# A depthwise convolution moved wholly to TensorE as 128x32 products over shifted copies

## The chip, the cores and the metric

The kernel runs on one core of one Trainium2 chip. The metric is the device time of one execution in microseconds (us). Lower is better.

## The reference

The program is a small network over 256 tokens of width 1024: ten stages, of which six are feed-forward blocks and four are mixers (a convolution with windowed attention, forgetting attention, an mLSTM, a relative-position attention). The change concerns the convolution in the second stage, the "even" mixer:

```
z = h @ w_in                                # h [256, 1024]
u, gate = z[..., :512], z[..., 512:1024]
a = u * sigmoid(gate)                       # [256 tokens, 512 channels]
y = causal depthwise conv of a, 31 taps, weights w [31, 512], + b
a_out = silu(layernorm(y) * ln_g + ln_b)
b_out = windowed attention of 8 heads, from q, k, v = z[..., 1024:]
h = concat(a_out, b_out) @ w_out
```

Depthwise means that channel c of the output sums 31 shifted copies of channel c alone, each with its own factor. Everything is float32.

## The kernel before

**Tiling.** Tokens come in two blocks of 128, b = 0 and b = 1. Weights stream from DRAM in units of 128x2048 float32 (1 MB) into two buffers named `raw`; ACT rounds each half of a unit to a high part and DVE subtracts to get a low part (both `hl`, 20 buffers of 128x1024, so five units). A product of activations and weights is three TensorE matmuls (high by high, high by low, low by high), issued 512 columns wide. Small products (attention scores, transposes, the convolution) are plain float32: in the profile such a matmul stands as two instructions, here called halves; a transpose is one.

**The order of the work.** Each operation is recorded with an engine, an estimated duration, the tiles that it reads and writes, and a key (the unit of weights it belongs to, plus offsets). `Rec.schedule` plays a list schedule over PE, ACT, DVE and the DMA queue: among what is ready on an engine it takes the lowest key, and tiles get buffers as they come free. The table `NUDGE` shifts the keys of single groups ("even conv b0 p" is the PE work of the convolution of block 0) and so sets the order by hand. What comes out is one fixed order for each engine; every engine then runs in that order and waits on semaphores. All DMAs of the kernel are issued from one queue, SP's, in order too.

**The convolution** (`Net.even`, lines 1098 to 1271). After the gate, `a` is transposed to channels by tokens and copied into `aT` (two tiles, each with two of the four groups of 128 channels, `ct`, and 30 columns of zeros ahead of the tokens). The number `cg=6` splits the work. Of group 0 all 31 taps and of group 1 the last 15 are done on TensorE: one 128x128 diagonal matrix for each tap, loaded from DRAM (`in_diag`, 12 loads), times the shifted tokens. That makes 46 products for each token block, 92 in all. The other 16 taps of group 1 and all of groups 2 and 3 are done on DVE: 78 instructions over 256 tokens each, a multiply and add by a factor per channel (lines 1173 to 1184). The results are `yT`, which the layer norm ("even ln") transposes back.

**What stands around it.** The same stage does the projections, scores, softmax and value products of eight attention heads, and its output projection follows with attention's half of the sum first. `L273` in the profile is every matmul, `L277` every transpose, `L281` every load, `L207` every ACT operation, `L217`, `L236` and `L248` are DVE's tensor-tensor, scalar-tensor-tensor and min-reduce helpers.

Of the kernel before, what the change touches and what calls it, by code (L numbers as in the profile page):

```python
# [12 lines left out]
P = 128  # L13
# [59 lines left out]
class Rec:  # L73
# [191 lines left out]
    def mm(self, out, l, r, start, stop, key=None):  # L265
        n = self.n_of(r)
        if r.v.dt == F32R:
            d = max(107.0 if self.shape(l)[1] > 64 else 53.5, n / 2.4) + 2.5
        else:
            ls = self.shape(l)  # L270
            d = 126.0 if ls[1] == 64 else 2 * max(107.0, n / 1.2) + 4
        self.op("PE", d, [l, r], [out],
                lambda: self.nc.tensor.matmul(self.res(out), self.res(l), self.res(r), start=start, stop=stop), key=key)  # L273

    def tr(self, out, in_, ident, key=None):
        self.op("PE", 109.0, [in_, ident], [out],
                lambda: self.nc.tensor.transpose(self.res(out), self.res(in_), self.res(ident)), key=key)  # L277

    def load(self, out, src, nbytes, key=None, after=None):
        o = self.op("DMA", max(nbytes / 360.0 + 0, 453.0), [src], [out],  # L280
# [179 lines left out]
class Net:  # L460
# [74 lines left out]
    def rstd(self, ss, w, n, key, more=False, cut=1):  # L535
        """[P, w] sums of squares (parts of them) -> rsqrt(ss / n + eps), Newton from the exponent trick"""
# [29 lines left out]
    def split_T(self, src, n, hi, lo, key, o0=0, pk=None):  # L566
        """transposes n [128,128] blocks of src into hi + lo at column block o0"""
# [10 lines left out]
    def ssq(self, b, key):  # L578
        """sums of squares of the halves of x"""
# [7 lines left out]
    def gain_T(self, b, g, key):  # L587
        """x * g, transposed and split"""
# [26 lines left out]
    def norm(self, b, g):  # L615
        """(x * g).T in two parts, and per token 1 / rms, half of it, half its square"""
# [9 lines left out]
    def mm3(self, out, x, w, first, last, key):  # L626
        """out += x.T @ w from halves: groups of one k-block"""
# [6 lines left out]
    def proj(self, b, xs, us, u0, n, per, grp=2):  # L634
        """bank [128, n] = x @ W; units hold `per` k-blocks of n columns each"""
# [16 lines left out]
    def oproj(self, b, acc, hi, lo, o0, un, u0, first, last):  # L652
        """acc[2 banks] += o @ W; unit holds 2 k-blocks of 1024 columns"""
# [13 lines left out]
    def postnorm(self, b, acc, g, scale):  # L667
        """x += scale * rmsnorm(acc) * g"""
# [138 lines left out]
    def bias_tile(self, b, name, j, key):  # L807
        """additive bias of 4 heads of a query block: for one key block or two"""
# [14 lines left out]
    def k_T(self, b, kT, pt, key):  # L823
        """bank [128, 2 pairs x 128] -> kT [128, 2 pairs x 256]"""
# [4 lines left out]
    def qk_T(self, b, key, bank, rs, kT, sgn=1.0):  # L829
        """row-layout bank [tok, 512] -> (qT [128, nq*128] scaled, kT) via transposes"""  # L830
# [13 lines left out]
    def logsig(self, z, w, out, key):  # L844
        """out = min(z, 0) - log1p(exp(-|z|)), [P, w]"""
# [29 lines left out]
    def gates(self, b, xs, gu, u0, key):  # L875
        """bank [128, 16] = x @ W for 16 columns: W is the stationary side, the sum is turned afterwards"""
# [221 lines left out]
    def even(self, gi):  # L1098
# [12 lines left out]
        cw, cbi, lg, lb = c[:, 520:644], c[:, 644:648], c[:, 648:652], c[:, 652:656]  # L1111
# [3 lines left out]
        T2 = 30 + 2 * P  # L1115
        a2 = [r.t("aT", 2 * T2, name="aT") for _ in range(2)]
        y = r.t("b4", name="yT")
        ng = [min(4, max(0, int(self.c["cg"]) - 4 * ct)) for ct in range(4)]
        part = [None, None]

        def tap(ct, t0, n):
            o = (ct % 2) * T2 + t0
            return a2[ct // 2][:, o:o + n]

        for b in range(2):
# [14 lines left out]
            for i in range(2):  # L1140
                if b == 0:
                    r.begin()
                    for ct in (2 * i, 2 * i + 1):
                        r.memset(tap(ct, 0, 30), 0.0)
                    r.end(key)
                r.begin()
                for ct in (2 * i, 2 * i + 1):
                    r.copy(tap(ct, 30 + b * P, P), pt[:, ct * P:(ct + 1) * P])
                r.end(key)
            r.lab = f"even conv b{b}"  # L1150
            kp = self.pos(b, u0 + 3) - self.c["vp"]
            for ct in range(4):
                if ng[ct] == 0:
                    continue
                bank = r.t("mm", name="cv")
                for q in range(4 - ng[ct], 4):
                    n = min(8, 31 - 8 * q)
                    d = r.t("b4", n * P, name="diag")
                    at = u0 + self.c["lead"] * b + self.c["du"] + 4 * ct + q
# [5 lines left out]
                ys = y[:, (2 * ct + b) * P:(2 * ct + b + 1) * P]  # L1165
                if ng[ct] == 4:
                    r.act(ys, bank[:, 0:P], AF.Identity, bias=cbi[:, ct:ct + 1], key=kp)
                else:
                    part[b] = r.t("b1", name="part")
                    r.act(part[b][:, 0:P], bank[:, 0:P], AF.Copy, key=kp)  # L1170
        r.lab = "even conv"
        key = self.pos(1, u0 + 3) - self.c["vb"]
        for j in range(31):
            r.begin()
            for ct in range(3, -1, -1):
                if j >= 8 * (4 - ng[ct]):
                    continue
                ys = y[:, 2 * ct * P:2 * (ct + 1) * P]
                w = cw[:, ct * 31 + j:ct * 31 + j + 1]
                if j == 0:  # L1180
                    r.ts(ys, tap(ct, j, 2 * P), w, cbi[:, ct:ct + 1], ALU.mult, ALU.add)
                else:
                    r.stt(ys, tap(ct, j, 2 * P), w, ys, ALU.mult, ALU.add)
            r.end(key)
        for ct in range(4):
            if 0 < ng[ct] < 4:
                for b in range(2):
                    ys = y[:, (2 * ct + b) * P:(2 * ct + b + 1) * P]
                    r.tt(ys, part[b][:, 0:P], ys, ALU.add, key=key)
# [37 lines left out]
        for b in range(2):  # L1227
# [4 lines left out]
            for j in range(4):  # L1232
                r.tr(pt[:, j * P:(j + 1) * P], y[:, (2 * j + b) * P:(2 * j + b + 1) * P], self.ident)
# [236 lines left out]
def _cols(w, c0, n):  # L1470
    """[1024, cols] -> units of n-wide columns, 2048 // n k-blocks each: [units, 128, 2048]"""
# [4 lines left out]
def _rows(w):  # L1476
    """[K, 1024] -> units of two k-blocks: [K / 256, 128, 2048]"""
# [11 lines left out]
def arrange(i):  # L1489
# [50 lines left out]
    diag = np.zeros((4, P, 32, P), np.float32)  # L1540
    cwt = i["conv_w"][0].reshape(31, 4, P)
    for c in range(4):
        diag[c, np.arange(P), :31, np.arange(P)] = cwt[:, c].T
# [4 lines left out]
        x=i["x"][0], w=np.concatenate(w), wg5=gates(fx, 3072 + np.array(slot)), wg7=gates(ml), cst=cst, row=row, swab=tile4(swab), diag=diag.reshape(4, P, 4096),  # L1548
# [7 lines left out]
    g=(F32, 1024, 3, 0), aT=(F32, 572, 4, 0), b4=(F32, 1024, 5, 0), b2=(F32, 512, 11, 0), b1=(F32, 256, 6, 0), s=(F32, 32, 16, 0),  # L1556
    acc=(F32, 512, 4, 1), mm=(F32, 512, 4, 1))
CFG = dict(lead=4, ahead=0, cb=2, fb=6, dd=4, ab=3, vb=2, ncst=784, stages=99, rk=3, bl=3, cg=6, vp=0, du=4, nd=0, k4=2, xb=1, k2=1)

NUDGE = {  # L1560
# [88 lines left out]
```

## Time and profile before

| | |
|---|---|
| median of 3 runs | 1593.0 us (1592.84 to 1593.87) |
| span of the profiled execution (its own time, first to last instruction) | 1591.4 us |
| PE busy | 1573.6 us (99%), clock granted at full in every slice |
| DVE, ACT busy | 1015.5 us (64%), 837.4 us (53%) |
| weights and other loads | 296.83 MB, 16 DMA engines 51% busy |

The profile counts an engine as busy from the start of an instruction to its end, and matmuls overlap each other by some hundred ns. So the price of one more matmul in a row is read from the growth of a row's length with its count, not from the mean duration. A timeline row merges instructions of one kind that follow each other: start, length, engine, line, what it writes and reads, count, and in brackets the idle time ahead of it with what ended it.

### The profile page before, as it was taken

The page shows a single profiled execution, that of the slowest core. Times are in us where ns is not written, and L with a number is a line of the kernel's source. Part 1 is how long each engine was busy: PE and PEld are TensorE (multiplying, and loading weights), DVE is VectorE, ACT ScalarE, POOL GpSimd, SP SyncE. Part 2 cuts the span into 40 slices and gives each one's busy share as a digit, 9 for nine tenths or more (in the row PEclk, how much of TensorE's full clock was granted, in tenths as well). Part 3 has the DMA queues.
Part 4 walks back from the last instruction along what each step waited for, and adds up shares of the span by engine and source line. Part 5 has one row for each costly group of instructions (what it writes and reads, how often), then busy time and mean ns, then how long its engine had stood idle before and what let it go on. Part 6 is the DMA issues. An engine that isn't in the chain of part 4 may idle for free.

```text
span 1591.4 us, 20430 instructions
## 1 busy us (share of the span) xinstructions
PE 1573.6 (99%) x7714; PEld 1289.5 (81%) x7714; DVE 1015.5 (64%) x1969; ACT 837.4 (53%) x1400; POOL 0.2 (0%) x4
## 2 busy tenths in 40 slices
PE   8999999999999999999999999999999999999998
PEld 6888888888888888887788888788888887788886
DVE  6555689854558555677964557887545576755544
ACT  6444556744455454566854445655444457754443
POOL 0000000000000000000000000000000000000000
PEclk9999999999999999999999999999999999999999
DMA  6655585355554555446444554445544645354542
GB/s 244 217 185 211 176 299 184 117 184 188 215 215 151 210 185 211 161 179 208 169 161 183 204 219 160 146 146 198 199 175 169 238 173 202 142 185 185 208 175 80
DMA packets 49587, 296.83 MB, mean 187 GB/s; under 512 B 5408, under 2 KB 8912, under 8 KB 16720
## 3 DMA queue, kind: packets, MB, share of 16 engines
q1 hardware_dynamic: 49488, 295.52, 50.9%
q8 instruction: 60, 0.98, 0.2%
q14 instruction: 39, 0.32, 0.1%
HBM read 294.43 MB, written 1.07 MB: 186 GB/s over the span
## 4 chain that ended last, share of the span: by engine, by line
PE 93%; DVE 3%; DMA 2%; ACT 1%; issue 0%; SPq 0%; ACTq 0%; DVEq 0%
PE mm L273 60%; PE acc L273 28%; PE mm L277 5%; DMA raw<-in_w 2%; DVE hl L217 1%; DVE b L236 1%; ACT hl L207 1%; ACT b L207 1%; DMA x<-in_x 0%; DVE s L236 0%; DVE xt L236 0%; DVE b L248 0%; ACT xt L207 0%; DVE x L236 0%; SPq L281 0%
## 5 line engine op out<-in xcount | busy, mean ns | idle before, releaser
L273 PE MATMUL mm<-hl,xt 128*128 128x512 f32 (+1 forms) x4224 | 1013.0, 393 | 0.6 <-DVE xt L217 0.3
L273 PEld LDWEIGHTS mm<-hl,xt 128*128 128x128 f32 x4224 | 778.0, 188 | 161.4 <-DVE hl L217 2.2
L217 DVE TENSOR_TENSOR hl<-raw,hl 128x1024 fp32r<-128x1024 f32 (+1 forms) x518 | 618.0, 1213 | 350.2 <-ACT hl L207 259.5
L207 ACT ACTIVATE hl<-raw 128x1024 fp32r<-128x1024 f32 (+1 forms) x518 | 522.3, 1048 | 332.6 <-DMA raw<-in_w 168.1
L273 PE MATMUL acc<-hl,gt 128*128 128x512 f32 x1584 | 385.8, 393 | 0.0
L273 PEld LDWEIGHTS acc<-hl,gt 128*128 128x128 f32 x1584 | 293.1, 188 | 59.4 <-ACT gt L207 0.2
L207 ACT ACTIVATE b<-mm,s 128x256 f32<-128x256 f32 (+2 forms) x188 | 94.0, 509 | 219.9 <-PE mm L273 214.7
L236 DVE SCALAR_TENSOR_TENSOR b<-mm,s,b 128x256 f32<-128x256 f32 x132 | 63.3, 481 | 98.4 <-ACT b L207 98.1
L277 PE MATMUL mm<-cst,b 128*128 128x128 f32 (+1 forms) x680 | 109.4, 272 | 3.0 <-DVE s L248 2.5
L277 PEld LDWEIGHTS mm<-cst,b 128*128 128x128 f32 (+1 forms) x680 | 85.4, 140 | 32.2 <-ACT b L207 3.7
L207 ACT ACTIVATE gt<-mm 128x256 fp32r<-128x256 f32 x132 | 50.0, 378 | 92.1 <-PE mm L277 84.6
L273 PE MATMUL acc<-hl,xt 128*128 128x512 f32 x384 | 96.0, 397 | 0.7 <-DVE xt L217 0.7
L217 DVE TENSOR_TENSOR gt<-mm,gt 128x256 fp32r<-128x256 f32 x132 | 55.2, 419 | 51.7 <-ACT gt L207 49.2
L273 PEld LDWEIGHTS acc<-hl,xt 128*128 128x128 f32 x384 | 70.0, 188 | 16.5 <-issue 1.4
L207 ACT ACTIVATE b<-b,s 128x128 f32<-128x128 f32 (+2 forms) x146 | 60.0, 442 | 15.0 <-DVE s L236 7.2
L236 DVE SCALAR_TENSOR_TENSOR s<-s 128x1 f32<-128x1 f32 (+2 forms) x260 | 47.8, 184 | 7.9
L207 ACT ACTIVATE b<-x 128x512 f32<-128x512 f32 x44 | 27.6, 628 | 23.0 <-DVE x L217 11.8
L207 ACT ACTIVATE xt<-mm 128x512 fp32r<-128x512 f32 x44 | 25.4, 595 | 22.0 <-PE mm L277 21.8
L236 DVE SCALAR_TENSOR_TENSOR b<-aT,cst,b 128x256 f32<-128x256 f32 x75 | 31.8, 477 | 0.0
L217 DVE TENSOR_TENSOR xt<-mm,xt 128x512 fp32r<-128x512 f32 x44 | 29.5, 685 | 3.0 <-ACT xt L207 2.4
L207 ACT ACTIVATE b<-mm 128x512 f32<-128x512 f32 (+4 forms) x44 | 21.5, 504 | 13.0 <-PE mm L277 11.2
L273 PE MATMUL mm<-aT,b 128*128 128x128 f32 (+1 forms) x232 | 28.2, 276 | 0.0
(75 smaller groups left out, 454.9 us busy)
## 6 DMA issues: line engine op xcount, KB each, us to landing
raw<-in_w SPq DMA_DIRECT2D x256, 1024.0 KB, 4.8
g<-in_gains SPq DMA_DIRECT2D x18, 512.0 KB, 6.2
b<-in_diag SPq DMA_DIRECT2D x8, 512.0 KB, 5.7
b<-dr SPq DMA_DIRECT2D x12, 256.0 KB, 5.3
g<-in_relb SPq DMA_DIRECT2D x4, 512.0 KB, 5.8
b<-in_diag SPq DMA_DIRECT2D x4, 448.0 KB, 5.3
x<-in_x SPq DMA_DIRECT2D x4, 256.0 KB, 5.3
raw<-in_w SPq DMA_DIRECT2D x4, 256.0 KB, 5.3
```

Source lines behind the costliest of these rows:

```text
L207: return self.nc.scalar.activation(self.res(out), self.res(in_), func, **kw)
L217: lambda: self.nc.vector.tensor_tensor(self.res(out), self.res(a), self.res(b), op), key=key)
L236: lambda: self.nc.vector.scalar_tensor_tensor(self.res(out), self.res(a), self.res(s), self.res(b), op0, op1, **kw), key=key)
L273: lambda: self.nc.tensor.matmul(self.res(out), self.res(l), self.res(r), start=start, stop=stop), key=key)
L277: lambda: self.nc.tensor.transpose(self.res(out), self.res(in_), self.res(ident)), key=key)
```

## The change

The convolution leaves DVE, and the diagonals go. For each token block, the four groups of 128 channels are each cut into four groups of 32 channels, `g`. A tile `taps` (it takes a buffer of the weight stream, `raw`) holds, for two of the channel groups, four copies of 32 channels on 128 partitions, copy q shifted by q tokens. Sixteen DMAs from `aT` fill one such tile; there are four tiles, so 64 DMAs. One product then does four taps of 32 channels: a stationary 128x32 matrix (four 32x32 diagonals above each other, from `in_cw`, four loads of 512 KB in all), 128 tokens moving, into 32 partitions of the result. Eight products make 32 taps (the last has weight zero), and the four `g` write the four quarters of the partitions: 32 products for each channel group and block, 256 in all. All four channel groups of a block share one PSUM bank, and DVE adds the bias in one operation per block.

Beside this the planner's estimates of PE durations are other numbers, and the table `NUDGE` is replaced throughout (226 entries before, 751 now), so the order changes in all ten stages.

```diff
     def mm(self, out, l, r, start, stop, key=None):
         n = self.n_of(r)
+        ls = self.shape(l)
         if r.v.dt == F32R:
-            d = max(107.0 if self.shape(l)[1] > 64 else 53.5, n / 2.4) + 2.5
+            d = n / 2.4 + (13.3 if ls[1] > 64 else 7.0)
+        elif ls[1] == 32:
+            d = 70.0
...
-    def load(self, out, src, nbytes, key=None, after=None):
-        o = self.op("DMA", max(nbytes / 360.0 + 0, 453.0), [src], [out],
+    def load(self, out, src, nbytes, key=None, after=None, dur=None):
+        o = self.op("DMA", dur or max(nbytes / 360.0 + 0, 453.0), [src], [out],
...
+        T2 = 32 + P
+        aT = [r.t("aT", 4 * T2, name="aT") for _ in range(2)]
+        v4 = lambda b: aT[b][:, :].rearrange("p (c t) -> p c t", c=4)
...
+            if b == 0:
+                r.memset(v4(0)[:, :, 0:30], 0.0, key=u0 - 6)
+            else:
+                r.dcopy(v4(1)[:, :, 0:30], v4(0)[:, :, P:P + 30], key=key)
+            r.memset(v4(b)[:, :, 30 + P:], 0.0, key=u0 - 6)
+            r.copy(v4(b)[:, :, 30:30 + P], pt[:, :].rearrange("p (c t) -> p c t", c=4), key=key)
...
-            for ct in range(4):
-                if ng[ct] == 0:
-                    continue
-                bank = r.t("mm", name="cv")
-                for q in range(4 - ng[ct], 4):
...
-                    r.load(d[:, :], self.a["diag"][ct][:, q * 1024:q * 1024 + n * P], P * P * 4 * n, key=at, after=self.near(at))
+            bank = r.t("mm", name="cv")
+            for h in range(2):
+                B = r.t("raw", 8 * 156, name="taps")
+                B4 = B[:, :].rearrange("p (c g t) -> p c g t", c=2, g=4)
+                r.begin()
+                for g in range(4):
+                    for q in range(4):
+                        r.load(B4[32 * q:32 * q + 32, :, g, :], v4(b)[32 * g:32 * g + 32, 2 * h:2 * h + 2, q:q + 156], 32 * 8 * 156, dur=110.0)
+                r.end(kp)
+                r.ops[-1].lat = 2000.0
+                for c_ in range(2):
+                    ct = 2 * h + c_
+                    w = cw[ct]
                     r.begin()
-                    for j in range(n):
-                        r.mm(bank[:, 0:P], d[:, j * P:(j + 1) * P], tap(ct, b * P + 8 * q + j, P), q == 4 - ng[ct] and j == 0, q == 3 and j == n - 1)
+                    for q in range(8):
+                        for g in range(4):
+                            o = (c_ * 4 + g) * 156 + 4 * q
+                            r.mm(bank[32 * g:32 * g + 32, ct * P:(ct + 1) * P], w[:, (4 * q + g) * 32:(4 * q + g + 1) * 32], B[:, o:o + P], q == 0, q == 7)
                     r.end(kp)
...
-        for j in range(31):
-            r.begin()
-            for ct in range(3, -1, -1):
...
-                    r.stt(ys, tap(ct, j, 2 * P), w, ys, ALU.mult, ALU.add)
-            r.end(key)
+            y = r.t("b2", name="yT")
+            r.tt(y[:, :].rearrange("p (c t) -> p c t", c=4), bank[:, :].rearrange("p (c t) -> p c t", c=4), cbi.unsqueeze(2).to_broadcast([P, 4, P]), ALU.add, key=kp)
...
 NUDGE = {
-    "F1 D10 b0 p": -1.75, "F1 D10 b1 p": -6.25, "F1 D3 b1 p": 0.25, "F1 D4 b0 p": -3, "F1 D4 b1 p": -2.25, "F1 D6 b0 p": -4.5,
+    "F1 D0 b0 p": 6.25, "F1 D0 b1 p": -0.25, "F1 D1 b0 p": 5.25, "F1 D1 b1 p": -9, "F1 D10 b0 p": -0.5, "F1 D10 b1 p": 14,
```

**What the engines do in a row there.** PE before, from the end of the key and value projection of block 1 on (`mm<-aT,b` is a row of tap products with diagonals, `mm<-cst,b` transposes, `mm<-b,b` attention scores, `acc<-b,b` value products):

```order
L273 MATMUL mm_196<-aT_129,b_136 128x128 x8
L277 MATMUL mm_193<-cst_68,b_153 128x128 x4
L277 MATMUL mm_194<-cst_68,b_162 128x128
L273 MATMUL mm_196<-aT_129,b_137 128x128 x8
L277 MATMUL mm_195<-cst_68,b_148 128x128 x4
L273 MATMUL mm_194<-b_161,b_154 128x256
```

The diagonals' rows of eight taps each stand between attention's, in nine such places up to the output projection.

PE now, from the same place (`mm<-raw,b` are the new products, 32 for one channel group of a block; `mm_194` collects block 1, `mm_193` later block 0):

```order
L279 MATMUL mm_194<-raw_76,b_136 32x128 x32
L283 MATMUL mm_195<-cst_68,b_152 128x128 x4
L283 MATMUL mm_196<-cst_68,b_149 128x128 x4
L283 MATMUL mm_193<-cst_68,b_153 128x128 x4
L279 MATMUL acc_188<-b_144,b_160 64x128 x4
L279 MATMUL acc_188<-b_151,b_160 64x128 x4
L283 MATMUL mm_195<-cst_68,b_162 128x128
L279 MATMUL mm_194<-raw_76,b_137 32x128 x32
L279 MATMUL mm_196<-b_161,b_147 128x256
```

Block 1 comes first. Its second pair of channel groups (`raw_77`) follows with attention's work between, then six matmuls of the output projection, and then block 0's four channel groups stand in one row of 128 products:

```order
L279 MATMUL acc_186<-hl_86,xt_104 128x512
L279 MATMUL mm_193<-raw_76,b_136 32x128 x32
L279 MATMUL mm_193<-raw_76,b_137 32x128 x32
L279 MATMUL mm_193<-raw_77,b_138 32x128 x32
L279 MATMUL mm_193<-raw_77,b_139 32x128 x32
L283 MATMUL mm_194<-cst_68,b_140 128x128 x4
```

So the convolution's PE work now stands in five stretches: 32, 32, 32, 32 and 128 products.

SP's queue now, around the same place:

```order
L287 DMA raw_77<-in_w 128x2048
L287 DMA b_150<-in_swab 128x4x128
L287 DMA g_124<-in_swab 128x1024
L287 DMA raw_76<-aT_130 32x2x156 x16
L287 DMA raw_77<-aT_130 32x2x156 x16
L287 DMA raw_76<-aT_129 32x2x156 x16
L287 DMA g_124<-in_swab 128x1024
L287 DMA raw_77<-aT_129 32x2x156 x16
L287 DMA raw_76<-in_w 128x2048
L287 DMA raw_77<-in_w 128x2048
```

Before, loads of weights and of diagonals stood mixed there:

```order
L281 DMA raw_77<-in_w 128x2048
L281 DMA b_136<-in_diag 128x1024
L281 DMA b_137<-in_diag 128x1024
L281 DMA b_152<-in_swab 128x4x128
L281 DMA g_124<-in_swab 128x1024
L281 DMA b_138<-in_diag 128x1024
```

Between two loads of weights the queue now issues 64 small DMAs for the taps, and both weight buffers are tap tiles meanwhile. At the program's head the queue now loads three quarters of the tokens before the first weights, where it alternated the two:

```order
L287 DMA cst_68<-in_cst 128x136
L287 DMA x_63<-in_x 128x512 x2
L287 DMA x_64<-in_x 128x512
L287 DMA raw_76<-in_w 128x512
L287 DMA x_64<-in_x 128x512
L287 DMA raw_76<-in_w 128x512 x2
```

The first weights stand after three token loads instead of after one.

## Rows read from the trace of the kernel before

**Rows 1.** The page, busy time of each engine and the granted clock in 40 slices.

```profile
PE 1573.6 (99%) x7714; PEld 1289.5 (81%) x7714; DVE 1015.5 (64%) x1969; ACT 837.4 (53%) x1400; POOL 0.2 (0%) x4
...
PEclk9999999999999999999999999999999999999999
```

**Rows 2.** Busy time by stretch: us, then each engine's us (count), clock, DMA share, GB/s.

```profile
0.00:40.00 40.00, 34.02 (x144) 26.82 (x145) 27.16 (x69) 25.09 (x49) 0.20 (x4) 1.00 0.67 245
...
200.00:240.00 40.00, 39.65 (x233) 34.27 (x232) 33.86 (x76) 20.23 (x34) 0.00 (x0) 1.00 0.81 298
240.00:280.00 40.00, 36.80 (x297) 32.20 (x296) 38.15 (x120) 28.00 (x75) 0.00 (x0) 1.00 0.49 182
280.00:320.00 40.00, 39.64 (x183) 31.98 (x182) 34.90 (x90) 29.18 (x56) 0.00 (x0) 1.00 0.34 117
320.00:1570.00 1250.00, 1249.78 (x6076) 1021.44 (x6075) 779.19 (x1460) 651.88 (x1066) 0.00 (x0) 1.00 0.50 184
```

**Rows 3.** PE's timeline in the convolution: start us, us, engine, line, what, count, idle before.

```profile
230.69 1.95 PE L273 MATMUL mm<-aT,b 128*128 128x128 f32 x16
...
232.59 5.30 PE L273 MATMUL mm<-aT,b 128*128 128x128 f32 x46
...
262.61 0.63 PE L277 MATMUL mm<-cst,b 128*128 128x128 f32 x4 [2.45 <-DVE s L248]
...
266.45 2.55 PE L273 MATMUL acc<-hl,xt 128*128 128x512 f32 x10 [0.75 <-DVE xt L217]
```

**Rows 4.** Groups of DVE and PE instructions by shape: us busy, mean ns | idle before.

```profile
L236 DVE SCALAR_TENSOR_TENSOR b<-aT,cst,b 128x256 f32<-128x256 f32 x75 | 31.8, 477 | 0.0
...
L273 PE MATMUL mm<-aT,b 128*128 128x128 f32 x184 | 22.2, 276 | 0.0
L273 PE MATMUL mm<-hl,xt 128*128 128x256 f32 x48 | 6.1, 283 | 0.0
```

**Rows 5.** PE's timeline, value products with 64 stationary columns, and what follows.

```profile
253.50 0.66 PE L273 MATMUL acc<-b,b 128*64 128x128 f32 x8
...
268.93 1.09 PE L273 MATMUL acc<-b,b 128*64 128x128 f32 x16
269.96 3.62 PE L273 MATMUL mm<-aT,b 128*128 128x128 f32 x30
```

**Rows 6.** SP's queue at the program's head: start us, us that one issue takes, what.

```profile
1.17 0.42 SPq L281 DMA_DIRECT2D x<-in_x  x1
1.64 0.42 SPq L281 DMA_DIRECT2D raw<-in_w  x1
2.11 0.43 SPq L281 DMA_DIRECT2D x<-in_x  x1
```

**Rows 7.** SP's queue in the convolution, the closest pair of issues.

```profile
226.10 0.33 SPq L281 DMA_DIRECT2D raw<-in_w  x1
226.47 0.44 SPq L281 DMA_DIRECT2D b<-in_diag  x1
```

**Rows 8.** DMA issues: KB each, median us from issue to landing.

```profile
raw<-in_w SPq DMA_DIRECT2D x256, 1024.0 KB, 4.8
...
out<-b SPq DMA_DIRECT2D x4, 256.0 KB, 2.1
...
raw<-in_wg SPq DMA_DIRECT2D x2, 64.0 KB, 2.6
cst<-in_cst SPq DMA_DIRECT2D x1, 68.0 KB, 1.9
dr<-b SPq DMA_DIRECT2D x3, 8.0 KB, 4.2
```

**Rows 9.** ACT's copy of one PSUM bank, as a group of its shape.

```profile
L207 ACT ACTIVATE b<-mm 128x512 f32<-128x512 f32 x28 | 16.2, 590 | 8.1 <-PE mm L277 7.6 <-DVE b L236 0.5
```

**Rows 10.** PE's timeline, rows of 512-column matmuls and of scores.

```profile
84.58 11.16 PE L273 MATMUL mm<-hl,xt 128*128 128x512 f32 x48
...
95.72 1.63 PE L273 MATMUL acc<-hl,gt 128*128 128x512 f32 x6
...
252.43 1.13 PE L273 MATMUL mm<-b,b 64*128 64x256 f32 x8
```

More of the change, by code (lines that the diff above doesn't have):

```diff
@@ L266, in mm @@
         n = self.n_of(r)
+        ls = self.shape(l)
         if r.v.dt == F32R:
-            d = max(107.0 if self.shape(l)[1] > 64 else 53.5, n / 2.4) + 2.5
-        else:
-            ls = self.shape(l)
-            d = 126.0 if ls[1] == 64 else 2 * max(107.0, n / 1.2) + 4
+            d = n / 2.4 + (13.3 if ls[1] > 64 else 7.0)
+        elif ls[1] == 32:
+            d = 70.0
+        elif ls[1] == 64:
+            d = 155.0
+        elif ls[0] == 64:
+            d = 117.0 + 0.766 * n
+        else:
+            d = 2 * max(112.0, n / 1.2)
         self.op("PE", d, [l, r], [out],
@@ L275, in tr @@
     def tr(self, out, in_, ident, key=None):
-        self.op("PE", 109.0, [in_, ident], [out],
+        self.op("PE", 109.0 + (20.0 if self.grp is None or self.grp.eng is None else 0.0), [in_, ident], [out],
                 lambda: self.nc.tensor.transpose(self.res(out), self.res(in_), self.res(ident)), key=key)
-    def load(self, out, src, nbytes, key=None, after=None):
-        o = self.op("DMA", max(nbytes / 360.0 + 0, 453.0), [src], [out],
+    def load(self, out, src, nbytes, key=None, after=None, dur=None):
+        o = self.op("DMA", dur or max(nbytes / 360.0 + 0, 453.0), [src], [out],
                     lambda: self.nc.sync.dma_start(self.res(out), self.res(src)), lat=2000.0, key=key)
@@ L1110, in even @@
         ou = [self.unit(u0 + 7 + i) for i in range(4)]
-        cw, cbi, lg, lb = c[:, 520:644], c[:, 644:648], c[:, 648:652], c[:, 652:656]
+        cbi, lg, lb = c[:, 644:648], c[:, 648:652], c[:, 652:656]
         nlg = r.t("s", name="nlg")
@@ L1114, in even @@
         kv, oT = [None] * 2, [None] * 2
[L1115 to L1123, printed above, removed]
+        T2 = 32 + P
+        aT = [r.t("aT", 4 * T2, name="aT") for _ in range(2)]
+        v4 = lambda b: aT[b][:, :].rearrange("p (c t) -> p c t", c=4)
+        yT, cw = [], []
+        r.lab = "even conv"
+        for ct in range(4):
+            cw.append(r.t("b4", name="cw"))
+            r.load(cw[ct][:, :], self.a["cw"][ct], P * 4096, key=u0 - 3 + ct, after=self.near(u0 - 3 + ct))
         for b in range(2):
@@ L1139, in even @@
             r.end(key)
-            for i in range(2):
-                if b == 0:
-                    r.begin()
-                    for ct in (2 * i, 2 * i + 1):
-                        r.memset(tap(ct, 0, 30), 0.0)
-                    r.end(key)
[L1146 to L1149, printed above, removed]
+            if b == 0:
+                r.memset(v4(0)[:, :, 0:30], 0.0, key=u0 - 6)
+            else:
+                r.dcopy(v4(1)[:, :, 0:30], v4(0)[:, :, P:P + 30], key=key)
@@ L1150, in even @@
+            r.memset(v4(b)[:, :, 30 + P:], 0.0, key=u0 - 6)
+            r.copy(v4(b)[:, :, 30:30 + P], pt[:, :].rearrange("p (c t) -> p c t", c=4), key=key)
             r.lab = f"even conv b{b}"
             kp = self.pos(b, u0 + 3) - self.c["vp"]
-            for ct in range(4):
-                if ng[ct] == 0:
-                    continue
-                bank = r.t("mm", name="cv")
-                for q in range(4 - ng[ct], 4):
-                    n = min(8, 31 - 8 * q)
-                    d = r.t("b4", n * P, name="diag")
-                    at = u0 + self.c["lead"] * b + self.c["du"] + 4 * ct + q
-                    r.load(d[:, :], self.a["diag"][ct][:, q * 1024:q * 1024 + n * P], P * P * 4 * n, key=at, after=self.near(at))
+            bank = r.t("mm", name="cv")
@@ L1164, in even @@
                     r.end(kp)
[L1165 to L1172, printed above, removed]
-        for j in range(31):
-            r.begin()
-            for ct in range(3, -1, -1):
[L1176 to L1182, printed above, removed]
-                    r.stt(ys, tap(ct, j, 2 * P), w, ys, ALU.mult, ALU.add)
-            r.end(key)
@@ L1185, in even @@
[L1185 to L1189, printed above, removed]
+            y = r.t("b2", name="yT")
+            r.tt(y[:, :].rearrange("p (c t) -> p c t", c=4), bank[:, :].rearrange("p (c t) -> p c t", c=4), cbi.unsqueeze(2).to_broadcast([P, 4, P]), ALU.add, key=kp)
+            yT.append(y)
         for b in range(2):
@@ L1232, in even @@
             for j in range(4):
-                r.tr(pt[:, j * P:(j + 1) * P], y[:, (2 * j + b) * P:(2 * j + b + 1) * P], self.ident)
+                r.tr(pt[:, j * P:(j + 1) * P], yT[b][:, j * P:(j + 1) * P], self.ident)
             r.end(key)
@@ L1539, in arrange @@
     tile4 = lambda m: np.ascontiguousarray(m.reshape(-1, 4, P, 2 * P).transpose(0, 2, 1, 3).reshape(-1, P, 1024))
[L1540 to L1543, printed above, removed]
+    cw = np.zeros((4, 4, 32, 8, 4, 32), np.float32)
+    cwt = np.concatenate([i["conv_w"][0].reshape(31, 512), np.zeros((1, 512), np.float32)]).reshape(8, 4, 4, 4, 32)
+    for k in range(32):
+        cw[:, :, k, :, :, k] = cwt[:, :, :, :, k].transpose(2, 1, 0, 3)
     ng = i["norm_g"]
@@ L1547, in arrange @@
     return dict(
-        x=i["x"][0], w=np.concatenate(w), wg5=gates(fx, 3072 + np.array(slot)), wg7=gates(ml), cst=cst, row=row, swab=tile4(swab), diag=diag.reshape(4, P, 4096),
+        x=i["x"][0], w=np.concatenate(w), wg5=gates(fx, 3072 + np.array(slot)), wg7=gates(ml), cst=cst, row=row, swab=tile4(swab), cw=cw.reshape(4, P, 1024),
         relb=tile4(rel), gains=gains)
@@ L1555 @@
     raw=(F32, 2048, 2, 0), hl=(F32R, 1024, 20, 0), xt=(F32R, 1024, 5, 0), gt=(F32R, 256, 8, 0),
-    g=(F32, 1024, 3, 0), aT=(F32, 572, 4, 0), b4=(F32, 1024, 5, 0), b2=(F32, 512, 11, 0), b1=(F32, 256, 6, 0), s=(F32, 32, 16, 0),
+    g=(F32, 1024, 3, 0), aT=(F32, 640, 4, 0), b4=(F32, 1024, 5, 0), b2=(F32, 512, 11, 0), b1=(F32, 256, 6, 0), s=(F32, 32, 16, 0),
     acc=(F32, 512, 4, 1), mm=(F32, 512, 4, 1))
-CFG = dict(lead=4, ahead=0, cb=2, fb=6, dd=4, ab=3, vb=2, ncst=784, stages=99, rk=3, bl=3, cg=6, vp=0, du=4, nd=0, k4=2, xb=1, k2=1)
+CFG = dict(lead=4, ahead=0, cb=2, fb=6, dd=4, ab=3, vb=2, ncst=784, stages=99, rk=3, bl=3, vp=0, nd=0, k4=2, xb=1, k2=1)
 NUDGE = {
[17 rows of a table removed]
-    "even attn b1": -2, "even attn b1 p": -5, "even conv": -6, "even conv b0 p": 10.5, "even conv b1 p": 14,
[22 rows of a table removed]
[62 rows of a table added]
+    "F8 post b1": -0.25, "even attn b0": -0.75, "even attn b1": 0.25, "even attn b1 p": -0.75, "even conv b0": 6.25,
[9 rows of a table added]
+    "fox gate b1": -2.5, "fox gate b1 p": -1, "fox norm b0": -7, "fox norm b0 p": -2.25, "fox norm b1": 1.5,
[51 rows of a table added]
 }
```

159 rows, old and new, of the table NUDGE are left out of this document.

## The prediction

> **What bounds the kernel now.** I read the page first: TensorE (PE) is busy 99% of the span at the full clock, DVE 64%, ACT 53% [rows 1]. So a microsecond counts only where it adds to PE's work or lets PE wait. The stretches show where PE waits at all [rows 2]: of the 1250 us from 320 to 1570 it is idle for 0.22, and in the convolution's neighbourhood, 200 to 320, for 0.35 + 3.20 + 0.36 = 3.9 us. The first 40 us hold 6.0 us of idle time. The timeline names the larger waits of the middle [rows 3]: 2.45 us for DVE's min-reduce and 0.75 us for DVE's split, in the stretch in which DVE is busy 38.15 of 40 us. So there is no slack to be won outside these places, and what the new order of the other nine stages can give is a few tenths; what it can lose I cannot read.
>
> The sum is made against the profiled execution, whose own time is its span, 1591.4 us; the median of 1593.0 lies 1.6 above it, and I add changes to the median.
>
> **What goes.** 92 products with diagonals are 184 halves [rows 4]. A row of 46 takes 5.30 us and one of 16 takes 1.95 [rows 3], so each further half costs (5.30 - 1.95) / 30 = 0.112 us: 184 x 0.112 = 20.6 us of PE. On DVE 78 operations go (75 of them 31.8 us, [rows 4]). They cost nothing by themselves, since PE hides DVE; but DVE's backlog is what the two waits above stand for, so I credit the whole 3.9 us and charge below what takes their place. ACT's copies and the 12 loads of diagonals were hidden under PE and count for nothing either way.
>
> **The new products.** 256 products are 512 halves, 32 columns wide, four of them side by side. No row shows that width. The nearest is the value product with 64 columns, two side by side: 16 halves take 1.09 us and 8 take 0.66 [rows 5], so (1.09 - 0.66) / 8 = 0.054 us for each, just half of 0.112. If four share as well as two, a half costs 0.028 and all cost 14.3 us; if it stays at 0.054, 27.6 us. I take 0.032, near the lower end because the first halving was complete: 512 x 0.032 = 16.4 us, a block of 32 products 2.05 us. The Trainium skill, "TensorE: Matmul & The Clock Gate", section "Measured speedup vs the span model", reports that three column tiles gave 2.38 and not 3; an estimate by that share (0.79) makes the products 18 us and the sum 1.7 us worse, and the 64-column row here does not show such a loss.
>
> A stretch of column-tiled work also costs at its ends: from 268.93 to the next row at 269.96 are 1.03 us for 16 halves, 0.16 over 16 x 0.054 [rows 5]. Five stretches: 0.8 us.
>
> **The taps on SP's queue.** This is the added wait. PE may start a block only when 16 DMAs have landed, and SP issues all 64 in order. Neighbouring issues stand 0.47 us apart at the head [rows 6] and 0.37 at the closest [rows 7], for transfers of any size; I take 0.42, so 16 take 6.7 us. Small transfers land in 1.9 to 2.6 us, with 4.2 for an 8 KB store [rows 8]; I take 1.9. A copy within the chip's memory is not in the trace. I count from T, the end of block 1's transposes:
> - ACT's copy to `aT` (0.59, [rows 9]) and the hand-overs: first issue at T + 1.0, landed at T + 1.0 + 6.7 + 1.9 = 9.6. PE has, by the new order, 18 matmuls of 0.227 ((11.16 - 1.63) / 42, [rows 10]), 24 of 0.127 [rows 4] and four score products of about 0.15: 7.7 us. **First wait 1.9.**
> - Block one ends at 11.7. Thirteen transposes, eight value products and their ends take 2.6, block two 2.05; with 0.6 for attention's softmax it ends at 17.0. The second set of taps landed at 1.0 + 13.4 + 1.9 = 16.3, no wait. The third set needs `raw_76` free: issue from 17.1 to 23.8, landed at 25.7. PE meanwhile does two sets of scores (1.07 each, [rows 10]), blocks three and four and six matmuls (1.36), and comes to 24.9. **Second wait 0.8.**
> - Blocks five and six: 4.1, to 29.8. The fourth set: 23.8, a load of 0.43 ahead of it in the queue, 6.7 and 1.9: 32.8. **Third wait 3.0.** PE ends at 36.9.
>
> That makes 5.7 us. Of the old waits on softmax and layer norm I keep 1.2. Behind the taps on SP stand the next weights: issue at about T + 31, landed 4.8 later [rows 8], split by T + 38, while PE has transposes, value products and 42 matmuls (some 15 us) from T + 37 before it needs them. That cover hides the gap; without it the gap would cost 1 us.
>
> **Head.** With the tokens first, PE does block 1's transposes early and both blocks share each split. Of 6.0 us idle I take 0.5 off, between 1.5 better and 1.0 worse.
>
> **Sum:** -20.6 - 3.9 + 16.4 + 0.8 + 5.7 + 1.2 - 0.5 = **-0.9 us, 1592.1 us.** The products save little, because the old ones were few; the waits for taps eat it.
>
> **The rivals.**
> 1. *The tap DMAs cost SP less than 0.30 us each.* Then 16 issues take under 4.8 us, all three waits vanish, and the sum is -6.6: **1586.4 us.** For it: these transfers are 40 KB on 32 partitions, smaller than nearly all others. Against: the issue of a 1 MB load takes 0.33 us [rows 7] and one of 256 KB 0.42 [rows 6], so the size does not set it, and no pair stands closer than 0.37.
> 2. *Slower: four groups do not overlap better than two.* At 0.054 a half the products take 27.6, 11.2 more; PE is then late itself, and the second and third waits (3.8) are hidden: +7.4, **1599.5 us.** The point from which this decides is about 0.043 a half. Against it: two groups halved the price completely. The same Trainium skill page, section "Wait — 56ns, not 53.3ns?", states some 62 ns of instruction handling for each MATMUL in one mode; by that 512 halves would take 31.7 us and the time would be near 1604. The trace's 54 ns is already below that figure, so I hold this mode to be off and give it 0.01 of this rival's chance.
> 3. *Slower: taps land late.* At 0.47 an issue and 3.0 to landing the first wait grows by 16 x 0.05 + 1.1 = 1.9, and the later ones, which build on SP's chain, by 32 x 0.05 + 1.1 = 2.7: +4.6 over the sum, **1596.7 us**; with landings of 4.2 as for the store [rows 8], 1599. From about 0.47 and 2.7 on the kernel is slower by over 0.2%.
> 4. *The new order stalls elsewhere*, on weights, or on ACT, where splits that wait for late weights stand ahead of copies PE needs: 3 to 6 us, about **1597 us**. For it: every key changed. Against: the old order left 0.22 us in 1250, made by the same planner.
>
> That the change does not do what it says is excluded by the order: 92 products out, 256 in, no tap on DVE.
>
> **How the numbers follow.** About 0.2% (3.2 us) is what a measurement of this kernel can tell from no change. Chances: my forecast 0.42 (of it 0.06 faster by over 0.2%, 0.34 within, 0.02 slower), the first rival 0.27 (0.26 faster, 0.01 within), the second 0.11 and the third 0.13 (0.22 slower, 0.02 within), the fourth 0.07 (0.06 slower, 0.01 within). Faster 0.32, same 0.38, slower 0.30. The range runs from the first rival, 1586, to the second, 1600: it leaves out 14.3 us for the products joined with cheap taps (1584) on one side and the worst of rivals two to four on the other. The forecast's own range, with 0.39 to 0.45 an issue and 0.028 to 0.037 a half, is 1589.5 to 1595.
>
> **What would show it.** Right: PE's timeline shows blocks of 32 products at about 2 us, with waits ahead of the first, fifth and seventh block ended by DMA `raw<-aT`; SP shows 64 issues some 0.4 us apart; the taps on DVE are gone, and so are its two waits; PE is idle for about 7 us between 200 and 320 and for some tenths from 320 on. Wrong: blocks of over 2.8 us (second rival); taps landing before PE arrives, without any such waits (first); waits that name weights or splits (fourth). If PE's total busy time does not fall by some 3 us beside these waits, the price of a half is the step that failed.

## The result, and the profile after

The changed kernel takes 1611.3 us (median of 4 runs, 1610.87 to 1613.07), the kernel before 1593.1: the ratio is 1.0113 (95% interval 1.0099 to 1.0128). It is 18 us slower, 19 above the forecast and outside its range. The span of the profiled execution is 1609.1 us.

The page of the changed kernel, answering to [rows 1]:

```profile
PE 1577.3 (98%) x8042; PEld 1290.0 (80%) x8042; DVE 987.5 (61%) x1891; ACT 838.3 (52%) x1390; POOL 0.2 (0%) x4
...
PEclk9999998999999999999999999999999999999999
```

PE is busy 3.7 us longer than before, although its work was to shrink, and one slice of the clock is no longer full. The stretches, answering to [rows 2], say where:

```profile
0.00:40.00 40.00, 33.35 (x138) 26.94 (x139) 26.17 (x65) 24.55 (x48) 0.20 (x4) 1.00 0.66 231
...
240.00:280.00 40.00, 27.32 (x465) 22.32 (x463) 6.37 (x29) 14.46 (x48) 0.00 (x0) 0.85 0.29 72
280.00:320.00 40.00, 37.08 (x299) 30.18 (x299) 27.66 (x67) 27.37 (x51) 0.00 (x0) 0.93 0.45 160
320.00:1570.00 1250.00, 1248.38 (x6077) 1021.47 (x6076) 789.36 (x1494) 658.02 (x1073) 0.00 (x0) 1.00 0.51 186
```

From 240 to 280 PE stands still for 12.7 us, where it stood for 3.2, and the granted clock of the stretch is 0.85: part of it was run at the lower level, 1.2 GHz. DVE is nearly idle there, as intended. In the 1250 us from 320 on 1.6 us are idle, against 0.2, and the first 40 us hold 6.65 us of idle time, against 5.98. PE's timeline in the convolution answers to [rows 3]:

```profile
242.72 0.41 PE L279 MATMUL mm<-raw,b 128*32 128x128 f32 x4
244.95 0.38 PE L279 MATMUL mm<-raw,b 128*32 128x128 f32 x2 [1.82 <-DMA raw<-aT]
247.39 3.33 PE L279 MATMUL mm<-raw,b 128*32 128x128 f32 x58 [2.06 <-DMA raw<-aT]
...
253.59 1.96 PE L279 MATMUL mm<-raw,b 128*32 128x128 f32 x64
...
259.07 1.91 PE L279 MATMUL mm<-raw,b 128*32 128x128 f32 x58 [2.12 <-DMA raw<-aT]
...
269.93 6.13 PE L279 MATMUL mm<-raw,b 128*32 128x128 f32 x124 [2.13 <-DMA raw<-aT]
276.58 0.38 PE L279 MATMUL mm<-raw,b 128*32 128x128 f32 x2 [0.52 <-DMA raw<-aT]
279.43 0.61 PE L279 MATMUL mm<-raw,b 128*32 128x128 f32 x2 [2.47 <-DMA raw<-aT]
281.59 5.42 PE L279 MATMUL mm<-raw,b 128*32 128x128 f32 x122 [1.55 <-DMA raw<-aT]
286.94 1.97 PE L283 MATMUL mm<-cst,b 128*128 128x128 f32 x16
```

A block of 64 halves that has its taps takes 1.96 us. Ahead of each pair of blocks PE waits, not once but up to three times, since the four groups `g` of a tile land one after the other. And 58 halves take 1.91 us in one place and 3.33 in another. Ahead of the fast row PE had waited once, 2.12 us; ahead of the slow one twice, 1.82 and 2.06 us with two halves between, and the granted clock of that row is 0.54. The rows of 6.13 and 5.42 us, behind two and three waits, have 0.59 and 0.66; the three rows of 64 or 58 halves that took 1.9 have 1.00. So each slow row was partly run at the lower level. All tap waits together are one row of the waits view (us in all, times, longest):

```profile
PE mm L279 <- DMA raw<-aT: 14.2, 8, 2.5
```

The cause stands in SP's timeline, which answers to [rows 6, 7]:

```profile
235.59 32.90 SPq L287 DMA_DIRECT2D raw<-aT  x48
268.60 0.53 SPq L287 DMA_DIRECT2D g<-in_swab  x1
269.23 10.94 SPq L287 DMA_DIRECT2D raw<-aT  x16
```

Forty-eight tap DMAs take SP 32.90 us, 0.685 each, without a gap; sixteen more take 10.94, 0.684 each. The transfers themselves are quick. Their row of the DMA issues answers to [rows 8] with the 1.9 us that the prediction took:

```profile
raw<-aT SPq DMA_DIRECT2D x64, 39.0 KB, 1.9
```

The four loads of `in_cw` carry 512 KB each, so 2 MB in all; no wait of PE names them.

### The profile page after: what moved, and what is told of

It reads as the page before. It is cut to its first block, busy times and chain, and to the rows that moved or that the text cites. A ratio compares the mean times of both kernels' runs of the same rounds, so it can differ in the third digit from the quotient of the medians.

```text
span 1609.1 us, 21039 instructions
## 1 busy us (share of the span) xinstructions
PE 1577.3 (98%) x8042; PEld 1290.0 (80%) x8042; DVE 987.5 (61%) x1891; ACT 838.3 (52%) x1390; POOL 0.2 (0%) x4
## 4 chain that ended last, share of the span: by engine, by line
PE 92%; DVE 3%; DMA 2%; SPq 2%; ACT 1%; issue 0%; DVEq 0%; ACTq 0%
PE mm L279 61%; PE acc L279 26%; PE mm L283 4%; SPq L287 2%; DMA raw<-in_w 2%; DVE hl L217 1%; DVE s L236 0%; DMA x<-in_x 0%; ACT b L207 0%; DVE b L236 0%; ACT hl L207 0%; DMA raw<-aT 0%; DVE x L236 0%; DVE xt L217 0%; DVE b L217 0%
## 5 line engine op out<-in xcount | busy, mean ns | idle before, releaser
L279 PE MATMUL mm<-hl,xt 128*128 128x512 f32 x4224 | 1010.0, 393 | 2.0 <-DVE hl L217 1.6
L283 PE MATMUL mm<-cst,b 128*128 128x128 f32 x680 | 108.4, 274 | 1.1 <-DVE b L217 0.9
L283 PEld LDWEIGHTS mm<-cst,b 128*128 128x128 f32 x680 | 83.9, 140 | 31.8 <-DVE b L217 2.4
L279 PE MATMUL mm<-raw,b 128*32 128x128 f32 x512 | 23.7, 335 | 14.2 <-DMA raw<-aT 14.2
L279 PEld LDWEIGHTS mm<-raw,b 128*32 128x32 f32 x512 | 20.0, 137 | 17.7 <-issue 17.4
L254 DVE COPY b<-mm 128x128 f32<-128x128 f32 (+3 forms) x56 | 16.8, 337 | 25.6 <-PE mm L283 21.4
L207 ACT ACTIVATE b<-mm 128x512 f32<-128x512 f32 (+3 forms) x42 | 20.8, 518 | 22.2 <-PE mm L283 22.0
```

The lines of the kernel that those rows point to most:

```text
L207: return self.nc.scalar.activation(self.res(out), self.res(in_), func, **kw)
L254: lambda: self.nc.vector.tensor_copy(self.res(out), self.res(a)), key=key)
```

## The experiments

Three theories went in. **S:** SP's queue sets the section; 64 issues of 0.685 us are a chain of 44 us, longer than the work PE has beside them. **O:** the new order loses by itself. **C:** the low clock after the waits is a cost of its own. Unless said otherwise, each kernel keeps the changed kernel's order on PE, ACT and DVE, instruction for instruction.

**No taps.** The tap DMAs are recorded for the planner but not issued:

```diff
-                        r.load(B4[32 * q:32 * q + 32, :, g, :], v4(b)[...], 32 * 8 * 156, dur=110.0)
+                        r.op('DMA', 110.0, [v4(b)[...]], [B4[32 * q:32 * q + 32, :, g, :]], lambda: None, lat=2000.0)
...
+                            r.fake = aT[b][:, ct * T2 + 4 * q:ct * T2 + 4 * q + P]
```

> The 64 tap DMAs are left out, and the 256 products read unshifted tokens of aT in place of the tap copies (so the convolution's values are not the reference's); the order on PE, ACT and DVE is that of the changed kernel. Theory S (SP's queue: 64 issues of 0.685 us in a row set the end of the section): the 14.2 us of waits for taps go, with them the 5.7 us that products took longer at the low clock, and of the 3 us of waits behind them (300 to 330) some: 1588 to 1592 us. Theory O (the new order loses by itself, on weights and softmax): most waits get other names, 1603 us or more. Theory P (the products are dear): PE's rows of 64 halves stay near 2 us and nothing changes but the waits, so as S; a row of over 2.5 us would speak for P.

Measured: 1586.9 us, ratio to before 0.9965 (0.9952 to 0.9978). PE's timeline in this kernel (line numbers are shifted; the products read `aT`):

```profile
242.77 1.96 PE L273 MATMUL mm<-aT,b 128*32 128x128 f32 x64
...
256.76 3.05 PE L273 MATMUL mm<-aT,b 128*32 128x128 f32 x104
260.02 4.36 PE L273 MATMUL mm<-aT,b 128*32 128x128 f32 x152 [0.21 <-issue]
264.31 1.96 PE L286 MATMUL mm<-cst,b 128*128 128x128 f32 x16
```

The first block starts where it did in the changed kernel (242.77 against 242.72), the products end at 264.31 instead of 286.94. So the taps cost 22.6 us there, and 24.4 in all (1611.3 - 1586.9). Order and products together, without the taps, are 6.2 us *faster* than the kernel before. O falls.

**Fewer pieces.** The tiles get the pitch of `aT`, so that a DMA moves 32 whole rows:

```diff
-                        r.load(B4[32 * q:32 * q + 32, :, g, :], v4(b)[32 * g:32 * g + 32, 2 * h:2 * h + 2, q:q + 156], ...)
+                        r.load(B[32 * q:32 * q + 32, g * 320:g * 320 + 316], aT[b][32 * g:32 * g + 32, h * 320 + q:h * 320 + q + 316], ...)
```

> Same 64 DMAs in the same places, but each moves 32 rows of 1264 bytes, where it now moves 64 pieces of 624. If the issue price goes with the pieces, it falls from 0.685 to 0.42 to 0.55 us, SP ends 9 to 17 us earlier, and the time is 1594 to 1602 us (theory S). If the price is one of each DMA, SP's row of 48 stays at 32.9 us and the time at 1611 us. Theory O: 1611 us either way.

Measured: 1609.8 us (1.011, 1.0095 to 1.0125). SP's timeline, the whole first row and the undisturbed part of it:

```profile
234.77 32.52 SPq L287 DMA_DIRECT2D raw<-aT  x48
...
234.77 7.56 SPq L287 DMA_DIRECT2D raw<-aT  x12
```

32.52 against 32.90 us: half the pieces change next to nothing. The price is one of each DMA. Undisturbed, that is in the first twelve issues, none of which stands out as longer than the others, it is 7.56 / 12 = 0.63 us.

**The same DMAs from DRAM.** To see whether it is the source that makes them dear, the DMAs of the last kernel read the input `x`:

```diff
-        lambda: self.nc.sync.dma_start(self.res(out), self.res(src))
+        lambda: self.nc.sync.dma_start(self.res(out), self.res(src) if xx is None else xx)
```

> The 64 DMAs of the run with 32 rows of 1264 bytes (e2), with the same shape and target, but read from the input x in DRAM instead of aT (so the convolution's values are not the reference's, and the DMAs no longer wait for aT). Only SP's price is asked: if 0.68 us goes with the source in the core's own memory, it falls to 0.33 to 0.47 as for weights and tokens; if it goes with the target of 32 partitions or with rows this short, it stays at 0.6 to 0.7.

SP's timeline, an undisturbed part (236.5 to 241.5) and the last set of sixteen:

```profile
236.21 5.49 SPq L287 DMA_DIRECT2D raw<-in_x  x12
...
258.43 8.32 SPq L287 DMA_DIRECT2D raw<-in_x  x16
```

The last set from `aT`, in the kernel with fewer pieces:

```profile
268.01 10.67 SPq L287 DMA_DIRECT2D raw<-aT  x16
```

Undisturbed 0.46 us each, where the same shape from `aT` took 0.63; over a whole set 0.52 against 0.67. So the source makes 0.15 to 0.17 of it, and the pieces make next to none. Why the source counts, no run shows. (Its one time, 1596.9 us, tells nothing of the change: its DMAs start 8 us earlier.)

**Half on GpSimd.**

```diff
-                    lambda: self.nc.sync.dma_start(self.res(out), self.res(src)), lat=2000.0, key=key)
+                    lambda: (eng or self.nc.sync).dma_start(self.res(out), self.res(src)), lat=2000.0, key=key)
...
+                        r.load(..., dur=110.0, eng=r.nc.gpsimd if q % 2 else None)
```

> Every second tap DMA is issued by GpSimd, whose queue is idle; order and sizes are those of the changed kernel. Theory S: SP's chain gets 32 x 0.685 = 21.9 us shorter; if GpSimd takes no more than SP for an issue, nearly all waits for taps vanish: 1589 to 1595 us. If GpSimd takes over 1.4 us for one, it becomes the chain, and nothing is won: 1611 us or more. Theory O: 1608 to 1611 us.

Measured: 1593.15 us (1.0003, 0.9993 to 1.0013), 18 us better with nothing changed but the queue. GpSimd's timeline has 16 issues in 8.55 us, 0.53 each:

```profile
234.49 8.55 POOL L287 DMA_DIRECT2D raw<-aT  x16 [234.04 <-ACT aT L207]
```

PE's timeline keeps three waits, all for the last tile, 1.75 us in all:

```profile
260.47 0.38 PE L279 MATMUL mm<-raw,b 128*32 128x128 f32 x2 [0.66 <-DMA raw<-aT]
261.53 0.38 PE L279 MATMUL mm<-raw,b 128*32 128x128 f32 x2 [0.68 <-DMA raw<-aT]
262.31 3.65 PE L279 MATMUL mm<-raw,b 128*32 128x128 f32 x122 [0.41 <-DMA raw<-aT]
```

The Trainium skill, "DMA: Bandwidth & Descriptors", section "Issuing engines are not separate DMA queues", says that a second issuing engine saves only the sequencer's time, "which is usually small relative to the DMA itself". Here it was not small: 44 us of a queue for transfers that land in 1.9, and moving half of it was worth 18.

**Half on ACT.** The same with `r.nc.scalar`.

> Every second tap DMA is issued by ACT instead of SP. Theory S: SP's chain is 21.9 us shorter, as with GpSimd (1593.2). But ACT has work of its own there: each of its four sets of 8 issues holds it for some 4 to 6 us, with softmax and layer norm behind it. If that is hidden, 1589 to 1594 us; if PE then waits for ACT, 1595 to 1603 us, and the waits are named ACT b, not DMA raw.

Measured: 1608.9 us (1.010, 1.0086 to 1.0113), worse than the worse case that was expected. ACT's timeline:

```profile
237.46 10.78 ACTq L287 DMA_DIRECT2D raw<-aT  x14
248.29 0.40 ACT L207 ACTIVATE b<-b,s 128x128 f32<-128x128 f32 x1 [11.14 <-DMA raw<-aT]
```

The softmax behind the issues waits 11.14 us, and PE's transposes for it:

```profile
250.38 1.35 PE L283 MATMUL mm<-cst,b 128*128 128x128 f32 x4 [4.85 <-ACT b L207]
```

The first tile comes earlier, but the wait changes its name, and the third set of taps, which needs the first tile's buffer, starts late again, and PE waits for taps once more at the end. Here splitting paid on the queue with nothing behind it and hardly on ACT's.

**Work in the waits.** Dummy matmuls, constants times constants into the bank that the products then overwrite:

```diff
+                            r.fill = (8 if b and h else 14) if c_ == q == g == 0 else 0
...
+                for _ in range(nf):
+                    self.nc.tensor.matmul(self.res(w), self.res(self.id_), self.res(self.id_), start=True, stop=True)
```

> The changed kernel with 14, 8, 14 and 14 idle matmuls (constants times constants, 0.224 us each at the high clock) ahead of the four pairs of blocks, so that PE works while it waits for taps. Theory S: the last taps land when they did; only the last pair of blocks, 5.42 us for 122 halves, comes down to some 3.7, so 1609 to 1611 us. Theory C (the low clock after each wait is a cost of its own, 5.7 us in all): 1605 to 1607 us.

Measured: 1610.1 us, ratio 1.0112 (1.0097 to 1.0127), where the changed kernel has 1.0113. PE's timeline:

```profile
246.35 1.91 PE L275 MATMUL mm<-raw,b 128*32 128x128 f32 x58 [1.38 <-DMA raw<-aT]
...
269.57 3.65 PE L275 MATMUL mm<-raw,b 128*32 128x128 f32 x122 [1.75 <-DMA raw<-aT]
...
281.07 6.39 PE L275 MATMUL mm<-raw,b 128*32 128x128 f32 x122 [1.58 <-DMA raw<-aT]
```

The rows that took 3.33 and 6.13 are back at the full clock (granted 1.00), and the last taps still come at 281. What the products win, PE waits for the next taps. So the slow time of these two rows, 3.9 us, lies inside SP's chain, and C falls for them. Only the last row could have gained, and it ran partly at the low clock here too (granted 0.61), after 2.14 and 1.58 us of waiting; what a fast last row would save, this run does not show.

**Through DRAM.** One store of `aT` for each token block, then four loads for each tile, 18 DMAs for 64:

```diff
+                if h == 0:
+                    r.load(dd, aT[b][:, :], 128 * 640 * 4, dur=594.0)
+                for q in range(4):
+                    r.load(B[32 * q:32 * q + 32, :].rearrange('p (g t) -> p g t', g=4)[:, :, 0:316],
+                           dd[:, h * 320 + q:h * 320 + q + 316].rearrange('(g p) t -> p g t', g=4), ...)
```

> The shifted copies come from DRAM: one store of aT (128x640) for each token block, then four loads for each pair of channel groups (32 partitions, four groups of 316 columns each), so 18 DMAs take the place of 64; the order on PE, ACT and DVE is that of the changed kernel. Theory S: SP issues a set in some 2 to 3 us, and no tap is late but for the trip through DRAM (the loads wait until the store has landed, 1.9 to 4.2 us): 1586 to 1590 us, as the kernel without taps at 1586.9. Rival D (the trip costs more than the issues it saves: store and loads, each with its landing, come to over 8 us ahead of the first block): first wait 2 us or more, 1591 to 1595 us.

Measured: 1587.6 us, ratio 0.9963 (0.9951 to 0.9976): it beats both kernels and stands level with the one without taps. SP's timeline:

```profile
234.56 0.33 SPq L287 DMA_DIRECT2D da<-aT  x1
236.79 3.65 SPq L287 DMA_DIRECT2D raw<-da  x8
240.49 0.43 SPq L287 DMA_DIRECT2D da<-aT  x1
248.52 2.11 SPq L287 DMA_DIRECT2D raw<-da  x4
...
254.41 2.05 SPq L287 DMA_DIRECT2D raw<-da  x4
```

Two tiles are issued by 240.4, though the loads wait some 2 us for the store; each load moves four times the bytes of a tap DMA for 0.46 us. PE's stretch from 240 to 280 is full, at the full clock:

```profile
240.00:280.00 40.00, 39.90 (x690) 33.94 (x690) 19.88 (x63) 28.75 (x73) 0.00 (x0) 1.00 0.58 180
```

and its timeline has block 0's 256 halves in one row, without a wait:

```profile
255.87 7.19 PE L279 MATMUL mm<-raw,b 128*32 128x128 f32 x256
263.00 1.97 PE L283 MATMUL mm<-cst,b 128*128 128x128 f32 x16
```

Rival D fell: the trip is hidden behind the projection's last matmuls. The Trainium skill, "DMA: Bandwidth & Descriptors", section "Rules for kernel authors", says to join many small transfers into one large one. The runs agree: 18 DMAs in place of 64 gave 1587.6 us for 1611.3.

**The planner told the price.** `dur=575.0` for 110.0, no other edit; with it the planner makes another order.

> The changed kernel with one number altered: the planner is told 0.685 us for each tap DMA (11 us a set) where it had 0.21 (3.4 us a set); DMAs and nudges stay, the planner alone reorders. Theory S: SP's chain of 64 issues ends where it did, near 280; what can change is what PE does meanwhile. If attention's products and the output projection's first half fill the waits, the 14.2 us of waits and the 5.7 at the low clock mostly go: 1592 to 1600 us. If the weights behind the taps on SP then run out, the wait moves to them: 1603 to 1611 us.

Measured: 1613.7 us (1.0133, 1.0116 to 1.015), above both expected ranges. PE's waits from 200 to 400, in the profiled execution, which at 1608.4 us was the shortest of four:

```profile
PE mm L283 <- DVE b L217: 6.4, 3, 5.3
PE acc L279 <- ACT xt L207: 4.2, 2, 2.4
PE mm L279 <- DMA raw<-aT: 3.9, 3, 2.2
```

The waits for taps fall from 14.2 to 3.9 us, and others come. The output projection's matmuls that now fill the tap waits are missing later, behind layer norm and the stage's last norm: PE waits for ACT's `xt` and, 5.3 us at once, for the tokens of the next stage. The wait moved, though not to weights as I wrote, and nothing was won. SP's chain is as long as before, 44.9 us from 233.71 to 278.58. This is one other order; whether a table of nudges made for the true price would cover the chain, no run shows.

**The order alone, both ways.** The kernel before under the new table and estimates, and the version through DRAM under the old table.

> The kernel before, with its diagonals and its taps on DVE, under the changed kernel's estimates and table of nudges: the new order alone. Theory S (the order is not what was lost): 1590 to 1598 us, the new table being made for other work. Theory O: 1603 us or more.

> The version that copies through DRAM (e5, 1587.6), under the table of nudges of the kernel before, so the new products in the old order as far as the planner gives it. If the new order is worth nothing by itself: 1586 to 1591 us. If it was needed for the new products, since the taps take the buffers of the weights: 1593 us or more. If the new order is a loss (theory O): under 1585 us.

Measured: 1613.6 us (1.0125, 1.0109 to 1.014) and 1641.7 us (1.0304, 1.0288 to 1.0319). Stretches of the first kernel:

```profile
280.00:320.00 40.00, 30.89 (x149) 23.00 (x147) 30.83 (x89) 26.68 (x60) 0.00 (x0) 0.87 0.14 53
320.00:1570.00 1250.00, 1249.62 (x6074) 1022.46 (x6073) 787.52 (x1493) 656.08 (x1069) 0.00 (x0) 1.00 0.50 185
```

The first number is the one that O had named, but its loss lies mostly in the convolution's own stage (9.1 us idle from 280 to 320, part of it at the low clock), whose work the table was not made for; from 320 on nothing is lost. The second says the same from the other side: 54 us worse than the same copies in the new order. Both orders were made for other work than they were given here, so these two runs do not tell what the new order is worth; the kernel without taps shows what order and products are worth together.

## Why the prediction was wrong

**What failed.** One term: "I take 0.42, so 16 take 6.7 us", under *The taps on SP's queue*. It was taken from issues that read DRAM [rows 6, 7], for DMAs that copy within the core's own memory, with the remark that no such copy was in the trace. The price was 0.685 on the mean, 0.63 where undisturbed. Of the 0.265 that were missing, some 0.15 come with the source. The other 0.1 would have been missing for DRAM too: those sixteen cost 0.52 each, and with 0.52 the chain below still gives some 10 us of delay (an estimate). The unknown was named and then bounded by 0.37 and 0.47. Those bounds were too narrow even for the trace of before, whose queue has longer issues in the convolution's own stretch:

```profile
234.95 0.56 SPq L281 DMA_DIRECT2D b<-in_swab  x1
235.55 0.68 SPq L281 DMA_DIRECT2D g<-in_swab  x1
```

A queue of 64 in a row multiplies such an error by 64.

**The chain itself was right.** Put 0.685 into it, with T set 1.0 before the first issue (235.59): 64 x 0.685 = 43.8, a load of 0.5, landing 1.9, so T + 47.2. PE's last row of products starts at 281.59, T + 47.0. By the same working, PE without waits reaches the last pair of blocks at T + 27.1 (24.9 less the first wait of 1.9, and 4.1 for blocks five and six), so the chain gives some 20 us of delay where I had 5.7. In the trace that delay is 14.2 us of waits and 5.6 us of slow rows: 58 halves in 3.33 instead of 1.91, 124 in 6.13 and 122 in 5.42 where the run from DRAM and the GpSimd run took 3.69 and 3.65. The other 2.8 of the 22.6 are mostly rows of 2 to 6 halves that start and drain by themselves between waits, 0.38 us for two. Two smaller things were off: the second set of taps, which the prediction had in time, made PE wait 2.12 us, and the 24.9 is a slip (17.0 + 2.1 + 4.1 + 1.4 is 24.6), which makes the predicted waits 6.0 and not 5.7.

**What the sum missed.** The clock had no term. As the filled kernel shows, it adds nothing in the first two slow rows, whose time lies inside SP's chain, but the last row, 122 halves in 5.42 us, ends the section and carries some 1.8 us of it. The Trainium skill, "TensorE: Matmul & The Clock Gate", section "HAM oscillation — how this bites in real kernels", describes products after DMA waits that start at the lower clock. The rows agree where two or three waits stood close together (granted 0.54, 0.59 and 0.66) and not behind the single wait of 2.12 us (1.00). And 1.8 us (24.4 - 22.6) are lost outside the convolution. Of them 1.3 show in the two traces, behind it: PE waits 0.20 us for ACT's `b` at 299.66, and at the next stage's first transposes for DVE's `b`, where the kernel without taps has no such waits.

```profile
314.89 1.26 PE L283 MATMUL mm<-cst,b 128*128 128x128 f32 x8 [0.76 <-DVE b L217]
```

The lag between the two kernels grows from 22.6 us at the end of the products to 23.95 here (314.89 against 290.94); the profiled spans differ by 24.0. The one wait of PE for split weights there (0.67 us, DVE's `hl` at 328.20) is there without taps too (0.68), so the cover named for late weights held.

**What was right, in part by luck.** The total of the other terms came out within a microsecond or so: the first rival, no wait for taps, was priced at 1586.4 us; without tap DMAs the chip gave 1586.9, and through DRAM 1587.6. Its terms were less exact and cancelled. The products were 2.4 us cheaper than taken: 192 further halves cost (263.00 - 255.87) - 1.89 = 5.24 us, 0.027 each against 0.032 (1.89 is the start-to-start time of a block of 64, 242.77 to 244.66 without taps). So four groups overlap as completely as two, and the second rival was wrong. Against that, the head did not get 0.5 better but 0.7 to 1.0 us worse (6.65 us idle in the changed kernel, 7.02 without taps, against 5.98), and from 320 on 0.5 to 1.0 us more were idle. The 1.9 us to landing was right. The third rival, late taps, was the mechanism, but its 0.47 an issue was far from enough, and the later landing that it joined to it did not come.

One of the prediction's signs pointed the wrong way. "If PE's total busy time does not fall by some 3 us" was to mean that the price of a half had failed. It rose by 3.7 us in the changed kernel, while that price was lower than taken: slow and short rows count as busy. Without the taps it fell by 5.9, to 1567.7.

## What to carry to other kernels

Count the DMAs that a change puts on one queue, and multiply by a price measured for that kind of source and target, before costing anything that waits for them: the queue is an engine with its own chain, and small copies filled it here at 0.46 to 0.69 us each. Where no row of that kind is in the trace, take the longest issue that is there as the bound. When this chain was too long, fewer DMAs helped (even by way of DRAM) and an idle queue helped, while the one other order that was tried and work put into the waits did not. A queue with work behind the issues mostly renamed the wait.

## What the runs showed of the hardware that was not expected

- A DMA within the core's own memory cost SP 0.63 us to issue, one of the same shape from DRAM 0.46. The number of pieces (64 of 624 bytes or 32 of 1264, from `aT`) and the size (40 or 158 KB, from DRAM) made no such difference. Why, the runs do not show.
- GpSimd issued the same DMAs in 0.53 us each, less than SP.
- A store to DRAM and loads back (landing in 3.5 and 3.2 us at the median) were faster for 16 shifted copies than 16 direct copies that land in 1.9 us each. By the rows above, the first tile takes some 7.3 us from the start of its store (2.2 to the loads, 1.8 for four issues, 3.2 to landing), and directly 16 x 0.63 + 1.9 = 12.0 (both estimates):

```profile
raw<-da SPq DMA_DIRECT2D x16, 158.0 KB, 3.2
da<-aT SPq DMA_DIRECT2D x2, 320.0 KB, 3.5
```

- Products of 32 stationary columns, four side by side, cost 0.027 us a half, a quarter of the 0.112 of a full-width one.
